# Four places of a two-layer backbone rewritten: key latents, adaLN rows and tanh moved, output weights asked for ahead, last tile scaled by two engines

## The chip, the cores and the metric

The kernel runs on one core of one Trainium2 chip. A core has five engines that run their own instruction lists and meet through semaphores: TensorE (PE: matmuls and transpositions), VectorE (DVE), ScalarE (ACT), GpSimd (POOL) and SyncE (SP), which here issues the DMAs. The metric is the device time of one execution in microseconds (us). All times are from the profiler's records or the timed runs.

## The reference

The program is one inference step of a diffusion backbone with two layers, on 256 context tokens (prompt) and 1024 latent tokens (sample), model width 1024. Cut to what matters:

```python
for l in (0, 1):
    shift, scale, gate = split(silu(cond) @ w_mod[l] + b_mod[l])     # "adaLN", for c_ctx and for c
    h = rmsnorm(y, norm_g[l]) * (1 + scale) + shift
    if l == 0:        # AB: windowed attention and a two-way matrix memory
        qa, ka, va, za, qb, kb, vb, ob, zb, gb = split(h @ w_in_ab)
        a = window_attention(rope(qa), rope(ka), va, cache, sink) * silu(za)
        qb, kb = split(silu(conv3([qb, kb])))                        # a centred convolution of 3 tokens
        b = norm(sigmoid(ob) * (memory_forward + memory_backward)) * silu(zb)
        out = concat(a, b) @ w_out_ab                                # 2048 x 1024
    else:             # C: attention over low-rank latents
        qa, kva, kr, z = split(h @ w_in_c)                           # 384, 256, 32, 1024 wide
        q = rmsnorm(qa) @ w_qb;  c_kv = concat(rmsnorm(kva), cache)
        k, v = split(c_kv @ w_kvb);  k = [k, rope(kr)]               # 16 heads
        out = (attention(q, k, v) * silu(z)) @ w_out_c               # 1024 x 1024
    y = y + gate * out
y_prompt, y_sample = rmsnorm(y, final_norm)                          # and the caches and states
```

## The kernel before

Matrices are kept as a high and a low half of an fp32 value (names ending in `h` and `l`), so that a product takes three matmuls: high by high, high by low, low by high. A product's weights are cast to the high half on ScalarE and the low half is a subtraction on VectorE or POOL. Tokens are handled in three chunks of 512, 512 and 256 (`CHUNKS`), or in ten tiles of 128 (`NT`).

The Python code lists the work; a scheduler that imitates the engines then lays out each engine's own order, and the order of each engine is fixed from there on. `K.later(f, n)` puts off a step by n steps of the surrounding flow, and `K.behind[(pass, tile)]` names what is to be issued beside a tile of a dense block. Memory on the chip is taken in pools, from a left and a right end (`left(...)`, `right(...)`); a new pool that lies over a released one waits for whoever last read there.

The places of the change, in the order of time:

- **adaLN rows** (`mod_sums`, line 501). Beside the first layer's work, the second layer's shift and scale are computed in blocks: 32 small matmuls, a ScalarE multiply into `mrow1` (L514, `mrow` in the profile), a transposition on PE, an addition on VectorE (L521).
- **The convolution of the memory branch** (`conv` in `b_proj`). ScalarE multiplies by the middle tap, VectorE adds the outer taps (L1629, L1630), ScalarE takes a tanh (L1632), VectorE finishes the silu (L1636), and the result `cx`, of which there are 4 buffers, is stored.
- **The output weights of layer AB** (`load_wout`, line 1009; `out_tile` uses them). They come one by one: a DMA on SP's queue, four steps later the cast (L1018) and the subtraction (L1019).
- **Key latents of layer C** (`kv_latent`, `k_rope`, `q_rope`, line 2020 on). `dense.run(2)` runs the last dense blocks of layer C's input product over the normalized input `hh0..2`, `hl0..2`. Query latents (`q_latent`) and the queries' rotary parts are placed beside it through `K.behind`. After it, the pool of the inputs is released, a pool `lat` is laid over it, and `kv_latent` for four chunks transposes the key latents and splits them into `ckv`, each with a `q_rope`.
- **Attention of layer C** (`Mla`). Eight pairs of heads; for each pair keys, queries and values are computed from `ckv`, the values of a pair into three tiles out of seven (`cV0` to `cV6`, three in the left pool `catt`, four in the right pool `cvr`). `SLOTS` says which: pair 7, the last, uses tiles 0, 2 and 1.
- **Output of layer C** (`weights_out`, `out`). The weights k = 0 to 2 go to a left pool (`cq`); before k = 3 the pools `cvr`, `ckv0`, `cw` and `lat` are released, and a pool `fin` over them takes k = 3 to 7 (`w`, L2183 and L2184), `fn`, `gate` and `o_x`. These steps and the first four output tiles are listed as filling for pair 7. An output tile is loaded (`o_a`), split (`o_ah`, `o_al`, L1056 and L1057), multiplied (48 matmuls), gated, added to `o_x`, squared and summed on ScalarE (L2205), and scaled by the root of the mean (L720, L721, L2216).

```python
SLOTS = ((3, 4, 5), (0, 1, 2), (3, 5, 0), (4, 6, 1), (0, 2, 4), (3, 5, 1), (4, 6, 3), (0, 2, 1))
```

Of the kernel before, what the change touches and what calls it, by code (L numbers as in the profile page):

```python
# [220 lines left out]
class Startup:  # L221
# [279 lines left out]
def mod_sums(K, p, blocks):  # L501


    nc, cond = K.nc, cond_cols(K, p)
    at = lambda t, c: t[c::32]
    if any(f < 2 * D for _, f in blocks):
        bcol = K.t(p, [128, 16], F32, "bcol1", 1)
        K.dma(bcol, K.I["k_cols"][:, 96:112])
        nc.vector.tensor_scalar(bcol[:, 8:16], bcol[:, 8:16], 1.0, None, ALU.add)
        K.A[1], K.Bm[1] = [K.const.tile([128, 2, 8], F32, tag=f"{n}1", name=f"{n}1") for n in "AB"]  # L510

    def columns(ps, f):
        rows = K.t(p, [128, 128], F32, "mrow1", 2)
        nc.scalar.mul(rows, ps[:, 0:128], 0.5)  # L514
        pc = K.psT()
        K.tr(pc[:, 0:128], rows)
        a, k = f // D, f % D // 128
        src = pc[:, 0:128].rearrange("p (q r) -> p q r", r=32)[:, :, 0:2]
        dst = (K.A if a else K.Bm)[1][:, :, k:k + 4].rearrange("p c k -> p k c")
        bc = lambda t, o: t[:, o + k:o + k + 4].unsqueeze(2).to_broadcast([128, 4, 2])  # L520
        nc.vector.tensor_add(dst, src, bc(bcol, 8 * a))  # L521
        if a:
            nc.vector.tensor_mul(dst, dst, bc(K.gcol, 8))

    def gate(ps, l, f, bias):
        nc.vector.scalar_tensor_tensor(bias, ps[:, 0:128], 0.5, bias, ALU.mult, ALU.add)
        for c in range(2):
            K.dma(K.modd[l][c, f:f + 512].rearrange("(q p) -> q p", p=128), at(bias, c))

    for l, f in blocks:  # L530
        ws, bias = [], None
        for i in range(8):
            for k in (2 * i, 2 * i + 1) if i < 4 else ():
                w = K.t(p, [128, 512], F32, "mw", 8)
                K.dma(w, K.I["w_mod"][l, k * 128:(k + 1) * 128, f:f + 512])
                ws.append(w)
            if i == 4 and f >= 2 * D:
                bias = K.t(p, [128, 128], F32, "bmod", 2)
                nc.gpsimd.memset(bias, 0.0)
                for c in range(2):  # L540
                    K.dma(at(bias, c), K.I["b_mod"][l, f:f + 512].rearrange("(q p) -> q p", p=128))
            if i == 7:
                ps = K.ps()
                for k in range(KD):
                    for q in range(4):
                        K.mm(ps[q * 32:q * 32 + 32, 0:128], cond[:, k, :], ws[k][:, q * 128:(q + 1) * 128], k == 0, k == KD - 1)
                if bias is None:
                    columns(ps, f)
                else:
                    gate(ps, l, f, bias)  # L550
# [299 lines left out]
def layer_ab(K):  # L850
# [158 lines left out]
def load_wout(K, p, src, ks, given=()):


    nc = K.nc
    K.wbufs = 2 * (len(ks) - len(given)) + (1 if len(ks) == 6 else 2)
    out = []

    def split(i, wf, half=None):
        wh, wl, wf = [t if half is None else t[:, half * 512:half * 512 + 512] for t in (*out[i], wf)]
        nc.scalar.copy(wh, wf)  # L1018
        (nc.gpsimd if K.flow or i % 3 else nc.vector).tensor_sub(wl, wf, wh.bitcast(F32))  # L1019

    def begin(i, wf):
        out.append(given[i] if i < len(given) else [K.t(p, [128, D], F32R, "w", K.wbufs) for _ in range(2)])
        if K.flow:
            split(i, wf, 0)
            K.later(partial(split, i, wf, 1))
        else:
            split(i, wf)

    for i, k in enumerate(ks):
        wf = K.t(p, [128, D], F32, "w", K.wbufs)  # L1030
        def ask(i=i, k=k, wf=wf):
            K.dma(wf, src[k * 128:(k + 1) * 128, :])
            K.later(partial(begin, i, wf), 4)

        K.later(ask, 1 + 3 * i)
    return out


# [556 lines left out]
def b_proj(K, wp, h):  # L1595
# [26 lines left out]
    def conv(p, ci, qk, j):  # L1622
        t0, N = CHUNKS[ci]
        cw = K.cw[:, :, qk * 8 + 2 * h + j]
        x = K.t(K.cvp, [128, 512], F32, "cx", 4)[:, 0:N]
        nc.scalar.mul(x, p[:, 1:N + 1], cw[:, 1:2])

        def taps():
            nc.vector.scalar_tensor_tensor(x, p[:, 0:N], cw[:, 0:1], x, ALU.mult, ALU.add)  # L1629
            nc.vector.scalar_tensor_tensor(x, p[:, 2:N + 2], cw[:, 2:3], x, ALU.mult, ALU.add)  # L1630
            th = K.sc(K.ring, [128, 512], F32, "cth")[:, 0:N]
            nc.scalar.activation(th, x, AF.Tanh, scale=1.0 if qk == 0 else 16.0)  # L1632
# [441 lines left out]
def layer_c(K):  # L2074
# [119 lines left out]
    def out(tt):  # L2194
        p = fin["p"]
        if tt in (0, 8):
            fin["gate"] = gate_row(K, p, 1, tt // 8)
        src = d["aT"][tt // 2][:, :, (tt % 2) * 128:(tt % 2) * 128 + 128]
        dst = K.O["y_sample"][0, tt * 128:(tt + 1) * 128] if tt < 8 else K.O["y_prompt"][0, (tt - 8) * 128:(tt - 7) * 128]
        ss = K.t(p, [128, 4], F32, "fss", 3)  # L2200
        if not tt:
            K.t(p, [128, 40], F32, "fpad", 1)

        def square(sl, y, x):
            nc.scalar.activation(x[:, sl], y[:, sl], AF.Square, accum_out=ss[:, sl.start // 256:sl.start // 256 + 1])  # L2205

        y = out_tile(K, p, [(src, 0, 4), (src, 4, 8)], fin["w"], fin["gate"], K.y2[tt], 4, square, fast=tt == NT - 1)
        if not tt:
            K.t(p, [128, 40], F32, "gpad", 1)
        nc.vector.tensor_add(ss[:, 0:1], ss[:, 0:1], ss[:, 2:3])  # L2210
        if tt == NT - 1:
            nc.vector.tensor_add(ss[:, 0:1], ss[:, 0:1], ss[:, 3:4])
        r = rstd_of(K, p, ss[:, 0:1], D, EPS, "fr")
        for n in range(0, D, 512):
            sl = slice(n, n + 512)
            nc.vector.scalar_tensor_tensor(y[:, sl], y[:, sl], r[:, 0:1], fin["fn"][:, sl], ALU.mult, ALU.mult)  # L2216
            K.dma(dst[:, sl], y[:, sl])
# [12 lines left out]
class Mla:  # L2230
# [298 lines left out]
```

## Time and profile before

| | us |
|---|---|
| median of three runs | 2583.2 (2578.94 to 2584.51) |
| the profiled execution | 2580.0 (2579.96) |
| its span in the profile | 2578.2 |
| PE busy in it | 2534.9 (98%) |
| mean granted PE clock | 0.996 |

The prediction shows the rows that it rests on. In the timeline a row is: start (us from the span's start), length, engine, line, operation, `out<-in`, shape, how many instructions were merged, and in brackets how long the engine stood idle just before and who released it. The page's waits are "engine tile line <- engine tile line: us in total, times, longest". A row of windows gives the length, the busy time of PE, PEld, DVE, ACT and POOL with the number of instructions, the granted PE clock, the DMA engines' mean busy share and GB/s.

### The profile page before, as it was taken

To read this page: it belongs to the slowest core of one execution; us is meant where nothing else is said; L and a number is where in the kernel's file an instruction comes from. 1 tells how busy PE (TensorE), PEld (TensorE's weight loads), DVE (VectorE), ACT (ScalarE), POOL (GpSimd) and SP (SyncE) were. 2 spreads that over 40 slices of the span, in tenths; PEclk is the share of its full clock that TensorE was granted. 3 is DMA by queue.
4 is the path that set the end of the run, shared out by engine and by line. 5 is a ranking of instruction groups with operands and counts; after the bars stand their busy time and mean duration, and the time that the engine had idled before them with its cause. 6 is when DMAs were issued, how large, how long until landed. Compare 5 with 4: busy or idle time off the path is not lost.

```text
span 2578.2 us, 48626 instructions
## 1 busy us (share of the span) xinstructions
PE 2534.9 (98%) x16482; PEld 2248.8 (87%) x16482; DVE 1702.8 (66%) x3927; ACT 1442.0 (56%) x3664; POOL 1126.9 (44%) x1510
## 2 busy tenths in 40 slices
PE   8999999999999999999999999999999999999998
PEld 6998998998998888878888778898899999999887
DVE  6633655656657575677777456426888888888754
ACT  6423535535434432577666433233888888888842
POOL 6223233233225344366554543135455555555832
PEclk9999999999999999999999999999999999999999
DMA  7665576666577564465443455423210101101334
GB/s 267 209 196 162 155 215 180 182 202 178 160 220 225 182 215 150 113 171 161 127 124 97 162 160 165 126 70 120 66 39 28 43 28 43 33 30 28 122 100 133
DMA packets 338955, 347.21 MB, mean 135 GB/s; under 512 B 36409, under 2 KB 281838, under 8 KB 338450
## 3 DMA queue, kind: packets, MB, share of 16 engines
q1 hardware_dynamic: 338706, 344.10, 43.8%
q8 instruction: 131, 2.15, 0.3%
q14 instruction: 118, 0.97, 0.1%
HBM read 233.49 MB, written 110.50 MB: 133 GB/s over the span
## 4 chain that ended last, share of the span: by engine, by line
PE 89%; DVE 3%; DMA 2%; ACT 2%; issue 2%; POOL 1%; SPq 1%; POOLq 0%; DVEq 0%; ACTq 0%
PE mm L119 36%; PE S L119 31%; PE V L119 9%; PE T L123 7%; PE D L119 3%; PE mm L123 3%; PE T L119 1%; SPq L154 1%; POOL w L1068 0%; DMA w<-in_w_out_c 0%; DMA w<-in_w_out_ab 0%; DMA y<-w 0%; POOL wl L577 0%; DMA xin<-in_x_sample 0%; DVE gM L1535 0%
## 5 line engine op out<-in xcount | busy, mean ns | idle before, releaser
L577 POOL TENSOR_TENSOR wl<-wf,wh 128x256 fp32r<-128x256 f32 (+2 forms) x272 | 222.8, 845 | 496.7 <-ACT wh L576 432.9
L119 PE MATMUL mm<-hTh,wh 128*128 128x512 f32 (+1 forms) x912 | 329.2, 361 | 0.9 <-DVE scr L821 0.9
L119 PE MATMUL mm<-hTh,wl 128*128 128x512 f32 (+1 forms) x912 | 324.7, 356 | 0.0
L119 PE MATMUL mm<-hTl,wh 128*128 128x512 f32 (+1 forms) x912 | 324.1, 355 | 0.0
L119 PE MATMUL S<-cK,cQ 96*128 96x512 f32 (+3 forms) x1248 | 301.6, 365 | 0.8 <-ACT cPb L2421 0.4
L2469 DVE TENSOR_TENSOR cpl<-T,cph 128x512 fp32r<-128x512 f32 x336 | 227.8, 684 | 36.3 <-ACT cph L2468 32.5
L119 PEld LDWEIGHTS S<-cK,cQ 96*128 96x128 f32 (+1 forms) x1248 | 192.5, 189 | 20.7 <-ACT cPb L2421 1.7
L2468 ACT CAST cph<-T 128x512 fp32r<-128x512 f32 x336 | 192.4, 589 | 29.1 <-PE T L123 15.7
L119 PEld LDWEIGHTS mm<-hTh,wl 128*128 128x128 f32 x912 | 171.4, 188 | 27.0
L119 PEld LDWEIGHTS mm<-hTh,wh 128*128 128x128 f32 x912 | 171.5, 188 | 23.8 <-DVE scr L821 1.1
L119 PEld LDWEIGHTS mm<-hTl,wh 128*128 128x128 f32 x912 | 171.7, 188 | 23.2
L2419 DVE TENSOR_REDUCE cmx<-S 128x1 f32<-128x512 f32 x256 | 172.9, 682 | 20.6 <-PE S L119 18.9
L119 PE MATMUL V<-cph,cV 128*128 128x256 f32 x672 | 177.3, 289 | 1.0 <-ACT cph L2468 0.9
L119 PE MATMUL V<-cpl,cV 128*128 128x256 f32 x672 | 171.9, 284 | 0.8 <-DVE cst L2396 0.3
L1343 ACT CAST att_ph<-mm 128x512 fp32r<-128x512 f32 x168 | 98.6, 587 | 94.4 <-PE mm L123 92.6
L2400 POOL TENSOR_SCALAR cPa<-cPa,cst 128x512 f32<-128x512 f32 x128 | 98.3, 768 | 114.5 <-DVE cst L2397 94.3
L119 PE MATMUL mm<-wh,hTh 128*128 128x256 f32 x480 | 136.2, 284 | 3.3 <-DVE scr L1649 3.2
L1344 DVE TENSOR_TENSOR att_pl<-mm,att_ph 128x512 fp32r<-128x512 f32 x168 | 115.8, 689 | 35.7 <-ACT att_ph L1343 30.8
L119 PE MATMUL mm<-wl,hTh 128*128 128x256 f32 x480 | 135.7, 283 | 0.1
L119 PE MATMUL mm<-wh,hTl 128*128 128x256 f32 x480 | 135.2, 282 | 0.0
L119 PEld LDWEIGHTS V<-cph,cV 128*128 128x128 f32 x672 | 126.6, 188 | 7.9 <-ACT cph L2468 1.1
L119 PEld LDWEIGHTS V<-cpl,cV 128*128 128x128 f32 x672 | 126.7, 189 | 6.7 <-DVE cpl L2469 0.9
(459 smaller groups left out, 7737.1 us busy)
## 6 DMA issues: line engine op xcount, KB each, us to landing
wf<-in_w_in_ab SPq DMA_DIRECT2D x120, 256.0 KB
in<-in SPq DMA_DIRECT2D x40, 514.0 KB
in<-in SPq DMA_DIRECT2D x32, 386.0 KB
mw<-in_w_mod SPq DMA_DIRECT2D x48, 256.0 KB
in<-scr SPq DMA_DIRECT2D x40, 258.0 KB
o_x<-y SPq DMA_DIRECT2D x20, 512.0 KB
xin<-in_k_wmod SPq DMA_DIRECT2D x16, 512.0 KB
in<-cx SPq DMA_DIRECT2D x32, 256.0 KB
```

The source lines that it names most:

```text
L119: return self.nc.tensor.matmul(out, lhsT, rhs, start=start, stop=stop)
L123: self.nc.tensor.transpose(out, in_, self.ident[:p, :p])
L154: self.nc.sync.dma_start(f(out), f(in_))
L577: K.nc.gpsimd.tensor_sub(wl, wf[:, k], wh.bitcast(F32))
L1343: K.nc.scalar.copy(ph, self.T)
L1344: K.nc.vector.tensor_sub(pl, self.T, ph.bitcast(F32))
L2400: nc.gpsimd.tensor_scalar(pv, pv, wt[:, c:c + 1], rd, ALU.mult, ALU.mult)
L2419: nc.vector.tensor_reduce(mx[:, b, c:c + 1], S, AX.X, ALU.max, negate=True)
L2468: nc.scalar.copy(ph, T_)
L2469: nc.vector.tensor_sub(pl, T_, ph.bitcast(F32))
```

## The change

1. `mod_sums` no longer transposes right behind ScalarE's multiply: the transposition and addition (`turned`) are kept and done when the next block has come to its third step.
2. The tanh of the convolution is put off by one step of the flow.
3. `load_wout` is a plain loop. It asks for two loads first and for one more ahead of each cast; the first load is on SP's queue, the others on ScalarE's.
4. Three of the four `kv_latent`, and eight `q_rope`, are spread beside the dense block. The pool `lat` is now the one that held `hh0` and `hl0`: the key latents are views of two tiles of their shape, and the fourth view of each becomes a value tile (`spare`). These are tiles 0 and 1 of the seven; three follow in `catt`, and `cvr` holds two.
5. In the last output tile the sums are folded into two small VectorE steps, and the second half is multiplied by `fn` on POOL beforehand, scaled on ScalarE and stored from ScalarE's queue.

```diff
@@ mod_sums
         nc.scalar.mul(rows, ps[:, 0:128], 0.5)
+        return partial(turned, rows, f)
+
+    def turned(rows, f):
         pc = K.psT()
         K.tr(pc[:, 0:128], rows)
...
+    late = None
     for l, f in blocks:
         ws, bias = [], None
         for i in range(8):
+            if i == 2 and late:
+                late = late()
...
-                    columns(ps, f)
+                    late = columns(ps, f)
...
+    if late:
+        late()
@@ dense blocks of layer C
+    K.lat = right("hT1")
+    hp = K.hp1 = right("hT2")
...
     for ci, (t0, N) in enumerate(CHUNKS):
+        hp = K.hp1 if ci else K.lat
@@ load_wout
+    nc, n = K.nc, len(ks)
+    K.wbufs = 2 * n + 1
+    out, raw = [], []
+
+    def ask(i):
+        if i < n:
+            raw.append(K.t(p, [128, D], F32, "w", K.wbufs))
+            (K.dma_act if i else K.dma)(raw[i], src[ks[i] * 128:(ks[i] + 1) * 128, :])
+
+    for i in range(2):
+        ask(i)
+    for i in range(n):
+        ask(i + 2)
+        wh, wl = [K.t(p, [128, D], F32R, "w", K.wbufs) for _ in range(2)]
+        out.append([wh, wl])
+        nc.scalar.copy(wh, raw[i])
+        (nc.gpsimd if i % 3 else nc.vector).tensor_sub(wl, raw[i], wh.bitcast(F32))
@@ conv
+            K.later(tanh)
+
+        def tanh():
             th = K.sc(K.ring, [128, 512], F32, "cth")[:, 0:N]
@@ layer_c
+    def keys_latent(ci):
+        if not ci:
+            for t, nm in zip(ckv, ("hh0", "hl0")):
+                whole = K.t(K.lat, [128, KD, 512], F32R, nm)
+                t += [whole[:, k:k + 2, :] for k in range(0, KD, 2)]
+        kv_latent(K, ci, ckv)
...
-    for n in range(8):
-        K.behind[1, n + 2] = [partial(q_rope, K, wr, n % 4, n // 4)]
-    K.behind[1, 5].append(partial(k_rope, K, 0))
-    K.behind[1, 9].append(partial(k_rope, K, 1))
+    for n, at in enumerate(((0, 7), (0, 8), (1, 0), (1, 2), (1, 3), (1, 4), (1, 6), (1, 8))):
+        K.behind.setdefault(at, []).append(partial(q_rope, K, wr, n % 4, n // 4))
+    for f, ci, at in ((k_rope, 0, (1, 5)), (k_rope, 1, (1, 9))):
+        K.behind.setdefault(at, []).append(partial(f, K, ci))
+    for ci, tt in ((0, 5), (3, 7), (1, 9)):
+        K.behind.setdefault((1, tt), []).append(partial(keys_latent, ci))
...
-    lp = right("lat")
-    ckv = [[lp.tile([128, 2, 512], F32R, tag=f"ckv{s}{c}", name=f"ckv{s}{c}") for c in range(3)] for s in range(2)]
+    lp = K.lat
+    spare = [t.pop().rearrange("p k (i g a d) -> p (k i) g a d", i=2, g=2, a=2) for t in ckv]
...
-    for ci in range(4):
-        kv_latent(K, ci, ckv)
-        q_rope(K, wr, ci, 2)
+    kv_latent(K, 2, ckv)
+    for q in range(4):
+        q_rope(K, wr, q, 2)
...
-    C.add_values(ap, sets[1])
+    C.add_values(ap, sets[1], spare=spare)
@@ out, last tile
+            if tt == NT - 1 and sl.start:
+                nc.gpsimd.tensor_mul(yf[:, sl.start - 512:sl.stop - 512], y[:, sl], fin["fn"][:, sl])
...
+            nc.vector.scalar_tensor_tensor(y[:, 0:512], y[:, 0:512], r[:, 0:1], fin["fn"][:, 0:512], ALU.mult, ALU.mult)
+            nc.scalar.mul(yf, yf, r[:, 0:1])
+            K.dma(dst[:, 0:512], y[:, 0:512])
+            K.dma_act(dst[:, 512:1024], yf)
@@ add_values
-        tiles = []
-        for pool, k in zip(pools, (3, 4)):
+        tiles = [*spare]
+        for pool, k in zip(pools, (3, 2)):
```

Since the scheduler sets the order, three places of the engines' orders show what moved.

PE, the first of the adaLN rows beside the first layer, before (`S` is a matmul's sum of a dense unit, `T` a transposition; the leading numbers of the names are buffers):

```order
L119 MATMUL S_1939<-wl_1484,hTh_127 128x256
L119 MATMUL S_1939<-wh_1483,hTl_128 128x256
L119 MATMUL S_1939<-wh_1487,hTh_127 128x256
L123 MATMUL T_2017<-ident,mrow_366_2015 128x128
L119 MATMUL S_1939<-wl_1488,hTh_127 128x256
L119 MATMUL S_1939<-wh_1487,hTl_128 128x256
```

and in the change:

```order
L119 MATMUL S_2076<-wh_1487,hTl_130 128x256
L123 MATMUL T_2106<-ident,mrow_366_2015 128x128
L119 MATMUL S_2113<-wh_1455,hTh_129 128x256
L119 MATMUL S_2113<-wl_1456,hTh_129 128x256
L119 MATMUL S_2113<-wh_1455,hTl_130 128x256
```

The transposition stands 38 rows later on PE, between two units. The two after it move by 38 and 26 rows, the fourth not at all.

SP's queue, the first of the last output weights, before (`caT` and `csz` belong to the gating of the attention's output; in brackets the engines and queues that a DMA waits for):

```order
L154 DMA caT_4176_19543<-csz_31419 128x256 [waits DMAHW4_49,Pool_49]
L154 DMA csz_31797<-csz_4172_19539 128x256 [waits DMAHW5_49,DMAHW4_49]
L154 DMA w_31947<-in_w_out_c 128x512 [waits DVE_49]
L154 DMA w_31974<-in_w_out_c 128x512 [waits DMAHW3_49,Activation_49]
L154 DMA w_32009<-in_w_out_c 128x512 [waits DMAHW0_49]
L154 DMA fn<-in_final_norm 128x1024 [waits DVE_49,PE_49]
L154 DMA gate_32362<-modd_54_144 128x1024 [waits DMAHW2_49]
L154 DMA o_x_32366<-y_0_469_2786 128x1024
L154 DMA w_32035<-in_w_out_c 128x512 [waits DVE_49]
```

and in the change:

```order
L154 DMA caT_4176_19546<-csz_32889 128x256 [waits Pool_49]
L154 DMA w_31941<-in_w_out_c 128x512 [waits DMAHW7_49,DVE_49,PE_49]
L154 DMA w_31968<-in_w_out_c 128x512 [waits PE_49]
L154 DMA w_32003<-in_w_out_c 128x512 [waits DMAHW1_49]
L154 DMA fn<-in_final_norm 128x1024
L154 DMA gate_32356<-modd_54_144 128x1024 [waits DMAHW3_49]
L154 DMA o_x_32360<-y_0_469_2786 128x1024 [waits DVE_49,PE_49]
L154 DMA w_32029<-in_w_out_c 128x512 [waits DMAHW5_49]
L154 DMA w_32062<-in_w_out_c 128x512 [waits DMAHW6_49,Activation_49]
L154 DMA o_a_32363<-caT_4173_19543 128x4x128 [waits DMAHW7_49]
```

Three loads now wait for PE: the first for values of pair 6 in `cV4`, the second for the matmuls of `V_33122` that read `hh_4699`, `o_x` for the last matmul of `V_33211` below. The store of `caT` ahead of them is that of pair 7's fourth tile, where before it was pair 6's.

PE at the end of the attention, in the change (`V` are the products with the values, of which `hh` and `hl` are the spare tiles; `mm<-cq,o_ah` is the first output tile):

```order
L119 MATMUL V_33122<-cph_33182,hl_4700_22307 128x256
L119 MATMUL V_33122<-cpl_33183,hl_4700_22307 128x256
L119 MATMUL V_33193<-cph_33199,hl_4700_22307 128x256
L119 MATMUL V_33193<-cpl_33200,hl_4700_22307 128x256
L119 MATMUL V_33211<-cph_33217,hl_4700_22307 128x256
L119 MATMUL V_33211<-cpl_33218,hl_4700_22307 128x256
L119 MATMUL mm_32375<-cq_31750,o_ah_32365 128x512
L119 MATMUL mm_32375<-cq_31751,o_ah_32365 128x512
L119 MATMUL mm_32375<-cq_31750,o_al_32366 128x512
```

All 480 matmuls of the output tiles stand behind the last `V` now. Before, 234 of the 480 stood among pair 7's attention, and the other 246 behind it.

More of the change, by code (lines that the diff above doesn't have):

```diff
@@ L962, in layer_ab @@
         opened.pop().release()
-    hp = K.hp1 = right("hT1")
+    K.lat = right("hT1")
+    hp = K.hp1 = right("hT2")
     K.hTh, K.hTl = [], []
     for ci, (t0, N) in enumerate(CHUNKS):
+        hp = K.hp1 if ci else K.lat
         K.hTh.append(hp.tile([128, KD, N], F32R, tag=f"hh{ci}", name=f"h1Th{ci}"))
@@ L1006, in place_wout, with load_wout @@
         yield
[L1009 to L1035, printed above, removed]
+def load_wout(K, p, src, ks):
+    nc, n = K.nc, len(ks)
[13 more added lines that the diff above has]
+        (nc.gpsimd if i % 3 else nc.vector).tensor_sub(wl, raw[i], wh.bitcast(F32))
     return out
@@ L2119, in layer_c @@
     K.u = {}
-    K.behind = {(0, 5): [partial(q_latent, K, 0)], (0, 9): [partial(q_latent, K, 1)], (1, 1): [partial(q_latent, K, 2)]}
-    for n in range(8):
-        K.behind[1, n + 2] = [partial(q_rope, K, wr, n % 4, n // 4)]
-    K.behind[1, 5].append(partial(k_rope, K, 0))
-    K.behind[1, 9].append(partial(k_rope, K, 1))
+    ckv = [[], []]
+    def keys_latent(ci):
[4 more added lines that the diff above has]
+        kv_latent(K, ci, ckv)
+    K.behind = {(0, 5): [partial(q_latent, K, 0)], (0, 9): [partial(q_latent, K, 1)], (1, 1): [partial(q_latent, K, 2)]}
+    for n, at in enumerate(((0, 7), (0, 8), (1, 0), (1, 2), (1, 3), (1, 4), (1, 6), (1, 8))):
[4 more added lines that the diff above has]
+        K.behind.setdefault((1, tt), []).append(partial(keys_latent, ci))
     dense.run(2)
@@ L2202, in out @@
             K.t(p, [128, 40], F32, "fpad", 1)
+        yf = K.t(p, [128, 512], F32, "fyf", 1) if tt == NT - 1 else None
         def square(sl, y, x):
             nc.scalar.activation(x[:, sl], y[:, sl], AF.Square, accum_out=ss[:, sl.start // 256:sl.start // 256 + 1])
+            if tt == NT - 1 and sl.start:
+                nc.gpsimd.tensor_mul(yf[:, sl.start - 512:sl.stop - 512], y[:, sl], fin["fn"][:, sl])
         y = out_tile(K, p, [(src, 0, 4), (src, 4, 8)], fin["w"], fin["gate"], K.y2[tt], 4, square, fast=tt == NT - 1)
@@ L2209, in out @@
             K.t(p, [128, 40], F32, "gpad", 1)
+        if tt == NT - 1:
+            nc.vector.tensor_scalar(ss[:, 2:3], ss[:, 2:3], ss[:, 0:1], D * EPS, ALU.add, ALU.add)
+            nc.vector.tensor_scalar(ss[:, 3:4], ss[:, 3:4], ss[:, 2:3], 1.0 / D, ALU.add, ALU.mult)
+            r = K.t(p, [128, 1], F32, "fr", 4)
+            nc.gpsimd.tensor_tensor(r, ss[:, 3:4], K.mhalf, ALU.pow)
+            nc.vector.scalar_tensor_tensor(y[:, 0:512], y[:, 0:512], r[:, 0:1], fin["fn"][:, 0:512], ALU.mult, ALU.mult)
+            nc.scalar.mul(yf, yf, r[:, 0:1])
+            K.dma(dst[:, 0:512], y[:, 0:512])
+            K.dma_act(dst[:, 512:1024], yf)
+            return
         nc.vector.tensor_add(ss[:, 0:1], ss[:, 0:1], ss[:, 2:3])
-        if tt == NT - 1:
-            nc.vector.tensor_add(ss[:, 0:1], ss[:, 0:1], ss[:, 3:4])
         r = rstd_of(K, p, ss[:, 0:1], D, EPS, "fr")
@@ L2250, in add_set, with add_values @@
         self.KV.append(keys)
-    def add_values(self, *pools):
+    def add_values(self, *pools, spare):
         n = 0
-        tiles = []
-        for pool, k in zip(pools, (3, 4)):
+        tiles = [*spare]
+        for pool, k in zip(pools, (3, 2)):
             tiles += [pool.tile([128, 4, 2, 2, 64], F32R, tag=f"cV{i}", name=f"cV{i}") for i in range(n, n + k)]
```

## The prediction

> **What bounds the kernel now.** I read the page first, then the waits of the tensor engine (PE), then single places in the timeline.
>
> ```profile
> PE 2534.9 (98%) x16482; PEld 2248.8 (87%) x16482; DVE 1702.8 (66%) x3927; ACT 1442.0 (56%) x3664; POOL 1126.9 (44%) x1510
> PE T L123 <- ACT mrow L514: 5.0, 2, 4.6
> PE mm L119 <- DVE scr L1649: 3.2, 1, 3.2
> PE T L123 <- DVE ckv L2071: 1.8, 4, 0.6
> ```
>
> PE is busy for 2534.9 of 2578.2 us. The change neither adds nor removes a matmul of any weight, so only what PE loses can move: idle time, the slower pace after it, and the end. The three waits shown (total, times, longest) are those that the edits aim at; a fourth is below.
>
> **The adaLN rows.** The transposition of `mrow` sat in the middle of a group of matmuls, and PE stood before it.
>
> ```profile
> 142.73 0.25 ACT L514 ACTIVATE mrow<-S 128x128 f32<-128x128 f32 x1
> 143.04 0.48 PE L123 MATMUL T<-ident,mrow 128*128 128x128 f32 x1 [4.59 <-ACT mrow L514]
> 143.74 0.41 PE L119 MATMUL S<-wh,hTh 128*128 128x256 f32 x1
> 143.95 0.41 PE L119 MATMUL S<-wl,hTh 128*128 128x256 f32 x1
> 149.03 0.28 PE L119 MATMUL S<-wh,hTl 128*128 128x256 f32 x1
> 149.14 0.28 PE L119 MATMUL S<-wh,hTh 128*128 128x256 f32 x1
> 147.33 1.27 ACT L1567 ACTIVATE rst<-rst 36x1280 f32<-36x1280 f32 x1
> 153.80 0.79 PE L123 MATMUL T<-ident,rst 36*128 36x36 f32 x10
> ```
>
> Two things were lost: 4.59 us of standing, and after it some 25 matmuls that started 0.21 us apart instead of 0.11 to 0.12, which is 25 x 0.094 = 2.3 us: 6.9 in all. Now 38 matmuls stand ahead of the transposition, 38 x 0.118 = 4.5 us, so PE reaches it at about 142.8, when `mrow` (142.98) is all but there. What is late next: the transposition of `rst` stood at 153.80 and comes 6.9 us earlier, at 146.9, but ScalarE's exponential ends at 147.33 + 1.27 = 148.60, and nothing in the edit moves that. PE waits some 2 us there; the gain is 153.80 - 148.8 = 5.0, less 0.3 for the restart: **4.7**, bounds 0 (the wait only moves) and 6.9.
>
> In the Trainium skill, "TensorE: Matmul & The Clock Gate" (Part 1: The HAM clock gate) has the array fall to half its clock after an idle window of about 3.4 us and come back after one busy window. The rows here agree in kind (0.21 against 0.11 to 0.12), though the slow stretch was longer, 143.04 to 148.65. By the page's window a wait of 2 us would not slow the array, and the sum would gain the 0.3 that I took off.
>
> **tanh one step later.** One wait, in a chain of four.
>
> ```profile
> 678.53 0.75 DVE L1630 SCALAR_TENSOR_TENSOR cx<-scr,cw,cx 128x512 f32<-128x512 f32 x1
> 679.32 0.63 ACT L1632 ACTIVATE scr<-cx 128x512 f32<-128x512 f32 x1 [0.75 <-DVE cx L1630]
> 680.24 0.42 DVE L1649 TENSOR_TENSOR scr<-mm,scr 128x256 fp32r<-128x256 f32 x1 [0.36 <-ACT scr L1648]
> 680.72 0.39 PE L119 MATMUL mm<-wh,hTh 128*128 128x256 f32 x1 [3.22 <-DVE scr L1649]
> ```
>
> The tanh waited for VectorE, and the cast and subtraction that free PE's bank stood behind it. With the tanh of the convolution before in its place, ScalarE is 0.75 us early; but the store of `cx` also goes one step later, and a later convolution reuses that buffer, so ScalarE's multiply must wait for the store. Of 3.22 us I take **1.1**; bounds -1 (that new wait is the longer one) and 4.9 (the wait and its slow pace both go). Elsewhere the 39 tanh's wait on ScalarE alone, and PE doesn't follow it.
>
> **The last output weights, asked for ahead.**
>
> ```profile
> 1456.99 8.73 DMA w<-in_w_out_ab
> 1476.45 1.05 ACT L1018 CAST w<-w 128x1024 fp32r<-128x1024 f32 x1 [6.00 <-DMA w<-in_w_out_ab]
> 1478.81 0.50 PE L119 MATMUL S<-w,o_ah 128*128 128x512 f32 x1 [0.30 <-DVE w L1019]
> 1483.12 0.50 PE L119 MATMUL S<-w,o_ah 128*128 128x512 f32 x1 [0.83 <-POOL w L1019]
> ```
>
> The loads landed one at a time, and PE paid 0.30 + 0.83 us, and in the matmuls around (0.50 us each against 0.39 at full pace, as below) about as much again. Asked two ahead, all six are under way earlier. But now ScalarE waits for a landing with the casts of `o_ah` behind it, and PE waits for those: up to 1 us. I take **1.5**, bounds -1 and 2.5. The Trainium skill ("Trainium Kernel Development and Optimization", Key Constraints) says that DMAs of several engines' queues run on the same 16 DMA engines, and that a second queue saves only the issuing time; no load here is issued by ScalarE before. By that rule the asking ahead alone would count, and this edit would bring nearer 0 than 1.5.
>
> **Key latents beside the dense block.**
>
> ```profile
> 1680.00:1740.00 60.00, 60.00 (x385) 59.00 (x384) 13.57 (x33) 25.11 (x64) 22.75 (x28) 1.00 0.29 70
> 1786.70:1801.00 14.30, 10.84 (x39) 7.34 (x38) 9.07 (x19) 7.63 (x17) 9.24 (x12) 0.76 0.51 157
> 1794.92 1.22 PE L119 MATMUL S<-ckv,wkh 128*128 128x512 f32 x2 [0.64 <-DVE cK L2068]
> 1798.50 0.63 PE L119 MATMUL mm<-cq,wql 128*128 128x512 f32 x1
> 1798.93 1.06 PE L119 MATMUL mm<-cq,wqh 128*128 128x512 f32 x2
> 1801.60 0.39 PE L119 MATMUL S<-ckv,wkl 128*128 128x512 f32 x1
> 1801.82 0.39 PE L119 MATMUL S<-ckv,wkh 128*128 128x512 f32 x1
> ```
>
> The first two rows are windows: length, busy us of PE, PEld, DVE, ACT and POOL, granted clock, DMA share and GB/s. In the 14.30 us of the second PE did 16 transpositions (0.11 each, about the step of the 256-column matmuls above) and 21 matmuls of 512 columns, which start 0.22 to 0.23 us apart at full pace (1801.60 to 1801.82): 1.8 + 4.8 = 6.6 us of work, so 7.7 were lost, to waits and to the slow pace (0.43 us from 1798.50 to 1798.93). Three of the four chunks now run among the dense block's matmuls, where PE was never idle (60.00 of 60.00) and VectorE and ScalarE had room; only the last keeps 4 transpositions here, with nine matmuls of `cq` as cover. **7.0**; bounds 4 (the last chunk still slows the clock) and 7.7.
>
> **The last tile.** After the last matmul came, in a row:
>
> ```profile
> 2572.74 0.16 DVE L2212 TENSOR_TENSOR fss<-fss 128x1 f32<-128x1 f32 x1 [0.57 <-ACT o_x L2205]
> 2573.82 1.42 DVE L2216 SCALAR_TENSOR_TENSOR w<-w,fr,fn 128x512 f32<-128x512 f32 x2 [0.73 <-POOL fr L721]
> 2574.60 1.00 SPq L154 DMA_DIRECT2D out_y_prompt<-w  x2
> ```
>
> One small VectorE step (0.2) goes; the second half is scaled and issued beside the first, half of 1.42 us and the second issue: **1.0**, bounds 0 and 2.
>
> **What the change puts in the way.** The key latents of chunk 0 stay in the old tile of `hh0`/`hl0`, and the spare quarter of each becomes a value tile. The last head pair reads them to the end, and the pool with the last output weights (`w<-in_w_out_c`, k = 3 to 7), `fn`, `gate` and `o_x` lies over that space. So the second of these loads waits for the last but one group of attention matmuls, `o_x` for the very last one, and the rest of SP's queue stands behind. In PE's order all 480 matmuls of the output come after the attention. Before, 234 of them were woven into it.
>
> ```profile
> 2401.90 1.37 SPq L154 DMA_DIRECT2D w<-in_w_out_c  x3
> 2404.74 9.24 DMA w<-in_w_out_c
> 2404.97 0.62 ACT L2183 CAST w<-w 128x512 fp32r<-128x512 f32 x1 [0.45 <-DMA w<-in_w_out_c]
> 2404.98 0.74 POOL L2486 TENSOR_TENSOR csz<-co,csz 128x256 f32<-128x256 f32 x1
> 2414.00 0.62 ACT L2183 CAST w<-w 128x512 fp32r<-128x512 f32 x1 [0.27 <-DMA w<-in_w_out_c]
> 2419.86 3.77 POOL L2184 TENSOR_TENSOR w<-w,w 128x512 fp32r<-128x512 f32 x3
> GB/s 0 0 125 0 166 259 283 254 244 285 218 339 367 390 380 359 226 312 46 183 70 12 2 232 16 0 0 47 78 45 265 231 82 0 0 23 212 28 11 0
> 2340.00:2404.00 64.00, 63.63 (x437) 57.29 (x435) 55.77 (x129) 57.30 (x159) 39.83 (x64) 1.00 0.15 44
> 2404.00:2435.00 31.00, 29.63 (x200) 26.23 (x201) 23.27 (x53) 27.72 (x74) 28.45 (x38) 1.00 0.54 171
> 2520.00:2571.00 51.00, 51.00 (x246) 42.54 (x245) 22.22 (x40) 12.04 (x29) 14.91 (x13) 1.00 0.44 146
> ```
>
> Attention without output matmuls keeps PE busy (63.63 of 64.00), so the new order costs nothing until the attention ends. Call that end t. The store that heads SP's queue follows a ScalarE copy (under the 0.62 of a cast twice as wide), a POOL product (0.74) and its issue, and begins from the group that ends 1 us before t: the first load is issued at about t + 1.2. The seventh issue, the second half of k = 4, came 2404.74 - 2401.90 = 2.8 us after the first and took 9.24 to land: t + 13.3. Its cast takes 0.62, and POOL's subtractions 3.77 / 3 = 1.26 each. The load of the first half of k = 7 must wait for the second of these (t + 16.4) for its buffer, then 3.1 us (2401.90 to 2404.97), 0.6 and 1.3: t + 21.5, and three matmuls more make t + 22.2. The 24 matmuls of that first group cost 24 x 0.225 = 5.4 us anyway: **PE loses 16.8**. To this come 1.2 for the last attention chain, which has no other work beside it, and 1.0 for a slow pace that POOL doesn't hide. Off goes 2.5 for the stretch 2404 to 2435, where loading disturbed the attention (29.63 busy of 31.00, and a slower pace). Sum: **a loss of 16.5**. Bounds: 10 if the loads, alone on the engines, land at the 390 GB/s that this stretch reached at best (the GB/s row, 40 slices from 2398 to 2440; the seven loads, four of 256 KB and three of 512, are 2.6 MB, 6.7 us instead of about 10.5), with the rest 2 us better for it, and 23 if the load of k = 7 takes 9.24 us instead of 3.1.
>
> **The sum.** Gains 4.7 + 1.1 + 1.5 + 7.0 + 1.0 = 15.3, loss 16.5: 1.2 us more than the profiled execution's own 2580.0 (span 2578.2), 2581.2. The median of the three runs is 3.2 us above that execution, which gives 2584.4; I take the middle, **2583**.
>
> **The rivals.**
> 1. *The loads land sooner* (faster). Nothing else uses the DMA engines after t. For it: the window 2404 to 2435 shows attention's own traffic beside the loads. Against it: 9.24 us from issue to landing came while the DMA engines were mostly this queue's. With a loss of 10 and all the gains: 2583 - 6.5 = 2576.5.
> 2. *The buffer decides* (slower). The load of k = 7 is asked for only when POOL has freed a buffer, and stands behind a load of `o_a` that waits for VectorE. It decides once that load takes over about 5 us to land. For it: POOL is the slowest link of the chain, and these loads landed in 3 to 9 us. Against it: by then little else is queued. Price 6.1: 2583 + 6 = 2589.
> 3. *The gains at the start and in the key latents are half* (slower). At both the stall may move to the next producer, as `rst` shows. 2583 + 6 = 2589 as well.
> 4. *The move does not bite*: the loads wait in SP's order, yet come before PE needs them, because attention ends late. The order speaks against it: the waits name the last matmuls. 2583 - 16.5 = 2566.5.
>
> **How the numbers follow.** Between two kernels here a difference under 0.2%, 5.2 us, can't be told from none. My forecast, no difference to be told, gets 0.42; the first rival 0.22 and the fourth 0.05; the second and third 0.31 together. So faster 0.27, same 0.42, slower 0.31. The forecast's own range is 2578 to 2588. The 8-in-10 range reaches to the first rival and to the second and third: **2573 to 2591**.
>
> **What would show it.** Right: at the end of attention PE idle for 12 to 15 us until `o_ah`, with the ten `w<-in_w_out_c` loads issued within some us behind it; no wait for `mrow` above 0.5 us; 1 to 2 us before `rst`; the stretch of the key latents 6 to 7 us shorter. Wrong: output loads issued some 100 us before the end as now, a wait of PE for a cast of `o_ah` near 1461, or new gaps among the dense matmuls before 1786.

## The result, and the profile after

| | before | the change |
|---|---|---|
| median | 2583.2 us (2578.94 to 2586.23, 5 runs) | 2607.88 us (2606.84 to 2609.08, 5 runs) |
| ratio, 95% interval | | 1.0099 (1.0084 to 1.0113) |
| span of the profiled execution | 2578.2 us | 2606.1 us |
| PE busy in it | 2534.9 us | 2537.9 us |

The change is 24.7 us slower, outside the range of the prediction (2573 to 2591). PE is busy for 3.0 us more than before, so of the 27.9 us between the spans 24.9 are idle time and the rest is slower pace. That kind of loss is what the prediction had; how much of it, and where, came out otherwise. One run of the kernel before, beside e5 to e7 below, took 10443.5 us and is in no ratio.

Rows of PE's waits, of the change (total us, times, longest):

```profile
PE mm L119 <- ACT o_ah L1059: 12.3, 1, 12.3
PE mm L119 <- DVE w L1070: 5.8, 7, 0.9
PE T L123 <- DVE B L524: 4.0, 1, 4.0
PE mm L119 <- DVE scr L1655: 3.5, 1, 3.5
PE V L119 <- DVE co L2513: 2.8, 3, 1.5
PE mm L119 <- DVE rp_t L829: 2.4, 1, 2.4
PE S L119 <- DMA mw<-in_w_mod: 1.9, 3, 0.9
PE S L119 <- POOL o_al L1432: 1.6, 1, 1.6
PE S L119 <- ACT o_ah L1431: 1.4, 1, 1.4
```

Of the three waits that the edits aimed at only `scr` is there in its old form (`mrow` is down from 5.0 to 0.4), and each has a successor: `mrow` became `B`, `ckv` became `rp_t`, the wait for the output weights `w` became two waits for `o_ah` and `o_al`. The first, second and fifth row are the end of the program, which had none of them before.

To see where the time went, the start of the same matmul is compared in both profiles. The table gives PE's lag behind the kernel before in us (minus: PE is ahead), worked out from the traces of the change and of the experiments below (e1 to e7), at places where the same work has been done:

| place (time before) | change | e1 | e2 | e3 | e4 | e5 | e6 | e7 |
|---|---|---|---|---|---|---|---|---|
| first transposition of the gates' rows (120) | +4.8 | +0.1 | +0.6 | +0.2 | +0.8 | -0.1 | +1.2 | +0.3 |
| gates done (183) | +4.6 | +1.7 | +0.3 | -1.0 | +0.4 | -3.2 | +0.2 | -3.0 |
| memory branch, behind the tanh place (732) | +5.5 | -0.3 | -1.6 | 0.0 | -1.4 | -2.9 | +1.7 | -3.0 |
| attention of the first layer ends (1445) | +5.7 | -0.1 | -1.5 | -0.9 | -1.2 | -2.9 | +1.3 | -1.5 |
| output of the first layer done (1640) | +4.8 | +2.3 | -0.7 | -2.7 | -0.8 | -3.7 | +0.9 | -3.2 |
| first keys by queries (1815) | -0.4 | -2.8 | -4.2 | -7.6 | -3.4 | -4.8 | -0.1 | -8.4 |
| second layer, early pairs (2132) | +2.9 | +1.8 | -1.1 | -4.2 | -0.4 | -4.6 | -0.1 | -6.2 |
| last matmul (2571) | +27.8 | +1.6 | +18.2 | -3.5 | +2.1 | -3.1 | -0.3 | -5.6 |

The first row is not the change's doing: up to that place the orders of PE and of SP's queue are the same in both kernels. In this one execution some `mw` loads came late (the row `mw<-in_w_mod` above); among the other eight profiles only e4 has such a wait, of 0.2 us. So of the 27.8 us, 4.8 are chance; whether the other four timed runs had such a delay isn't known. On the way from there to 2132 the change won 1.9 (4.8 to 2.9), not the 14 that I had summed. e2 has the same orders in this stretch, and e1 too but for the numbers of two value tiles: e2 won 1.7 in it, and e1 lost 1.7. Together the three show no gain clear of chance. The rest, 24.9, came behind 2132, all of it at the end.

**The end.** Two windows of the change there, then its timeline: SP's queue, ScalarE, POOL, PE and VectorE:

```profile
2434.00:2466.00 32.00, 28.70 (x222) 26.72 (x220) 25.08 (x58) 24.11 (x64) 15.16 (x27) 1.00 0.08 24
2466.00:2478.00 12.00, 0.05 (x1) 0.05 (x1) 0.49 (x2) 3.85 (x8) 6.07 (x6) 0.50 0.97 325
2464.47 1.34 SPq L154 DMA_DIRECT2D w<-in_w_out_c  x3
2475.71 1.33 ACT L2200 CAST w<-w 128x512 fp32r<-128x512 f32 x2 [5.11 <-DMA w<-in_w_out_c]
2477.28 0.62 ACT L1059 CAST o_ah<-o_a 128x512 fp32r<-128x512 f32 x1 [0.24 <-DMA o_a<-caT]
2476.41 7.12 POOL L2201 TENSOR_TENSOR w<-w,w 128x512 fp32r<-128x512 f32 x5 [4.46 <-ACT w L2200]
2483.89 1.28 POOL L2201 TENSOR_TENSOR w<-w,w 128x512 fp32r<-128x512 f32 x1 [0.36 <-ACT w L2200]
2477.95 1.22 PE L119 MATMUL mm<-cq,o_ah 128*128 128x512 f32 x2 [12.28 <-ACT o_ah L1059]
2485.52 0.62 PE L119 MATMUL mm<-w,o_ah 128*128 128x512 f32 x2
2486.45 0.69 DVE L1070 TENSOR_TENSOR w<-mm,gate 128x512 f32<-128x512 f32 x1 [5.31 <-PE mm L119]
2487.20 0.73 PE L119 MATMUL mm<-cq,o_ah 128*128 128x512 f32 x2 [0.84 <-DVE w L1070]
2493.86 0.70 PE L119 MATMUL mm<-cq,o_ah 128*128 128x512 f32 x2 [0.88 <-DVE w L1070]
```

The output loads go out at 2464.47, where before it was 2401.90, and PE stands for 12.28 us until the first `o_ah` is cast. That is what the prediction described. The output tiles are 504 matmuls by the trace (48 of the last tile are half as wide), not 480; before, 258 of them stood among the attention and 246 behind it, and now all stand behind. What the prediction had not: after each group of 24 matmuls PE pauses again, until VectorE has multiplied the sum by `gate` and so emptied the bank (L1070). The first four output tiles use the one bank of the pool `mm`. While their matmuls stood among the attention, other work covered this; now there is none, seven times.

### The profile page after: what moved, and what is told of

The parts are those of the page before. It is cut to its first block, busy times and chain, and to the rows that moved or that the text cites. A ratio compares the mean times of both kernels' runs of the same rounds, so it can differ in the third digit from the quotient of the medians.

```text
span 2606.1 us, 48638 instructions
## 1 busy us (share of the span) xinstructions
PE 2537.9 (97%) x16482; PEld 2250.5 (86%) x16482; DVE 1698.4 (65%) x3925; ACT 1441.1 (55%) x3665; POOL 1131.9 (43%) x1512
## 4 chain that ended last, share of the span: by engine, by line
PE 85%; DVE 3%; DMA 2%; issue 2%; ACT 2%; POOL 1%; SPq 1%; POOLq 0%; ACTq 0%; DVEq 0%
PE mm L119 34%; PE S L119 30%; PE V L119 9%; PE T L123 7%; PE D L119 3%; PE mm L123 3%; PE T L119 1%; SPq L154 1%; DMA o_a<-bT 0%; DMA o_a<-caT 0%; DVE cmx L2448 0%; DVE w L1070 0%; DVE att_pl L1347 0%; DMA out_new_cache_a_k<-scr 0%; DVE att_nm L1321 0%
## 5 line engine op out<-in xcount | busy, mean ns | idle before, releaser
L1335 POOL TENSOR_SCALAR att_p<-att_p,att_den 128x640 f32<-128x640 f32 (+1 forms) x128 | 97.9, 780 | 80.3 <-DVE att_den L1332 27.5
L584 ACT CAST wh<-wf 128x256 fp32r<-128x256 f32 (+2 forms) x272 | 96.2, 409 | 60.3 <-DMA wf<-in_w_in_c 24.0
L119 PE MATMUL V<-cph,cV 128*128 128x256 f32 x464 | 123.6, 289 | 0.0
L119 PE MATMUL V<-cpl,cV 128*128 128x256 f32 x464 | 119.3, 284 | 0.8 <-DVE cst L2422 0.3
```

Source lines behind the costliest of these rows:

```text
L119: return self.nc.tensor.matmul(out, lhsT, rhs, start=start, stop=stop)
L584: K.nc.scalar.copy(wh, wf[:, k])
L1335: nc.gpsimd.tensor_scalar(pv, pv, den[:, i:i + 1], 1.0, ALU.mult, ALU.mult)
```

## The experiments

The kernel before was run again beside each set, with medians of 2580.5 (e1 to e4) and 2582.4 us (e5 to e7); the ratios are to those.

**e1: the value tiles elsewhere.** One line of the change:

```diff
-        tiles = [*spare]
+        tiles = []
         for pool, k in zip(pools, (3, 2)):
             tiles += [pool.tile([128, 4, 2, 2, 64], F32R, tag=f"cV{i}", name=f"cV{i}") for i in range(n, n + k)]
             n += k
+        tiles[3:3] = spare
```

> The change with one line moved: the two spare value tiles are numbers 3 and 4 of the seven instead of 0 and 1, so that the last head pair (tiles 0, 2, 1) has all its values in the left pool and nothing of it under the pool of the output weights. Theory (that overlap is the tail's loss): the output loads are issued some 100 us before the end again, more than 200 of the 480 output matmuls stand among the last pair's attention, the 12.3 us wait for o_ah and the waits for DVE L1070 go; 2607.9 - 27.9 = 2580, between 2576 and 2585. Rival (the moved latents and the new pool layout as such delay the end): above 2600.

Measured: 2580.6 us, ratio 1.0001 (0.9991 to 1.0010). The first of the output loads on its SP queue, and all of PE's waits behind 2400:

```profile
2403.50 1.33 SPq L154 DMA_DIRECT2D w<-in_w_out_c  x3
```

```profile
PE V L119 <- ACT cph L2498: 0.9, 1, 0.9
PE V L119 <- DVE cpl L2499: 0.3, 1, 0.3
PE T L123 <- DVE cpl L2499: 0.2, 1, 0.2
```

The loads are 61 us earlier than in the change, and 12.3 + 5.8 + 2.8 us of waits are gone. They are issued 176 us before the end of the program, where the expectation had said some 100, and 258 of the output matmuls stand among the attention again. With the same moved latents, the whole loss goes with the place of two tiles. The rival falls.

**e2: three banks for the output tiles**, all else as in the change:

```diff
-               (24, partial(out, 0)), (29, partial(out, 1)), (34, partial(out, 2)), (39, partial(out, 3))])
+               ])
     C.finish()
     K.ps = K.psS
-    for tt in range(4, NT):
+    for tt in range(NT):
         out(tt)
```

> The change, with the first four output tiles taking their sums from the three banks of S, as the other six do, instead of the single bank of mm. Theory (seven pauses of PE after the attention are waits for VectorE to empty that one bank, 0.78 to 0.88 us each and about 1.0 with the restart): 2607.9 - 7 = 2601, between 2599 and 2604; the 12.3 us wait for o_ah stays. Rival (the pauses are the arrival of weights or the slow clock): within 2 us of 2607.9.

Measured: 2598.35 us, ratio 1.0074 (1.0057 to 1.0091), where the change had 1.0099: against the kernel before, 17.8 us in place of 24.7, so 6.9 less. That is 0.65 us below the stated range, which was reckoned from 2583.2 for the kernel before, while beside e2 that kernel took 2580.5. PE's waits from 2440 on:

```profile
PE S L119 <- ACT o_ah L1059: 13.5, 1, 13.5
PE V L119 <- DVE co L2513: 2.8, 3, 1.5
PE T L123 <- DVE cpl L2498: 0.2, 1, 0.2
```

The seven pauses are gone and the wait for `o_ah` stays. By the table e2 loses 19.3 us behind 2132, against 24.9. So the one bank is some 6 to 7 us of the loss, as the theory has it, and the rival falls.

**e3 and e4: the key latents alone, and all the rest alone.** e3 is the kernel before with the latents' part of the diff and the tile numbers of e1; e4 is the change without that part.

> The kernel before with the key latents' move alone, the spare value tiles as numbers 3 and 4. Theory (5.1 us are won up to the first product of keys and queries, and about 3.2 of it is given back in new waits for queries and keys behind it): 2583.2 - 1.9 = 2581, between 2577 and 2585. Rival (the term of the prediction holds, 7.0): 2576.

> The change without the key latents' move: adaLN rows, tanh, output weights asked ahead and last tile. Theory (the wait for mrow only moves to the transposition of rst, which waits for its bank; tanh costs about 1; the weights and the last tile bring nothing): 2583.2 + 1 = 2584, between 2580 and 2588. Rival (the terms of the prediction, 4.7 + 1.1 + 1.5 + 1.0): 2575.

Measured: e3 2580.57 us, 0.9997 (0.9988 to 1.0007); e4 2583.39 us, 1.0011 (1.0002 to 1.0021). Neither reaches the prediction's terms. Of e4's lag of 2.1 us at the last matmul, 2.5 is one wait for a cast of `cph` at 2408.79, a place that its edits don't touch. The table shows where e3's gain goes: from -2.7 at 1640 (up to there e3 has no edit, so that is chance) to -7.6 at the first keys by queries (4.9 won, 7.0 predicted), and back to -4.2 at 2132. The waits that take it back, in the change:

```profile
1797.26 0.70 PE L119 MATMUL mm<-cq,wqh 128*128 128x512 f32 x2 [2.43 <-DVE rp_t L829]
1822.78 0.47 PE L119 MATMUL mm<-hh,wkh 128*128 128x512 f32 x1 [1.45 <-DVE cQ L2074]
```

2.43 us remain at the old place, since the last rotary part still goes through VectorE before PE can go on, and another 1.45 come where the attention starts. Both stand in e3 as well. e4 leaves the latents where they were. Its window over the old place, and its own wait at the start of the attention:

```profile
1786.70:1801.00 14.30, 10.73 (x50) 7.50 (x50) 8.82 (x18) 7.82 (x18) 8.45 (x11) 1.00 0.53 168
1819.70 0.44 PE L123 MATMUL T<-ident,cPa 128*128 128x128 f32 x2 [1.45 <-POOL cPa L2416]
```

It had won 2.6 us from 1640 to the first keys by queries, too (-0.8 to -3.4), with the same four waits for `ckv` as before (1.8 us) but a granted clock of 1.00, where the kernel before had 0.76: that gain goes with the clock. It gave 3.0 back by 2132. So the profiles that gain between 1640 and the start of the attention wait there; e5, whose lead is older, keeps it (-4.8 to -4.6). What sets that pace stays open.

**e5: the adaLN rows behind the gates**, on the kernel before:

```diff
-            if i == 2 and late:
+            if i == 4 and late:
```

> The kernel before with the adaLN rows alone, but put off to the next block's fifth step instead of its third, so that the transposition of mrow stands on PE behind the three of the gates (LI, rst, gM) and not ahead of them. Theory (in the change the transposition of rst waits, beyond ScalarE's exponential, for the bank that the transposition of mrow left full: its emptying, L524, stands on VectorE behind four subtractions that wait for ScalarE's casts): rst then waits for the exponential alone, PE stands some 2 us there, and PE's lead over the kernel before behind the gates is 4 to 5 us, where it is 0 in the change; the time is 4 to 5 us below the kernel before. Rival (PE cannot be early there at all, because the gate chain on VectorE sets the pace): no lead behind the gates, and no difference in time.

Measured: 2578.57 us, 0.9985 (0.9976 to 0.9994): 3.8 us below. The two kernels at the transposition of `rst`, first the change:

```profile
152.15 1.27 ACT L1570 ACTIVATE rst<-rst 36x1280 f32<-36x1280 f32 x1
153.99 1.42 ACT L1654 CAST scr<-S 128x256 fp32r<-128x256 f32 x5
154.09 1.41 DVE L1655 TENSOR_TENSOR scr<-S,scr 128x256 fp32r<-128x256 f32 x4
155.49 0.16 DVE L524 TENSOR_TENSOR B<-T,bcol 128x8 f32<-128x8 f32 x1
155.80 1.25 PE L123 MATMUL T<-ident,rst 36*128 36x36 f32 x10 [4.02 <-DVE B L524]
```

and e5:

```profile
147.24 1.27 ACT L1575 ACTIVATE rst<-rst 36x1280 f32<-36x1280 f32 x1
148.56 0.81 PE L123 MATMUL T<-ident,rst 36*128 36x36 f32 x10 [1.78 <-ACT rst L1575]
```

In the change the exponential of `rst` was done at 153.42, but PE went on at 155.80, when VectorE had emptied the bank of `mrow` (L524), behind four subtractions, behind ScalarE's casts. With the transposition put behind the gates, PE waits 1.78 us for the exponential and nothing else. PE's lead behind the gates is 3.2 us (3.0 in e7), a little below the 4 to 5 expected. The theory holds, with its size somewhat too large; the rival falls.

**e6: one queue**, for the output weights and the last tile of the change on the kernel before:

```diff
-            (K.dma_act if i else K.dma)(raw[i], src[ks[i] * 128:(ks[i] + 1) * 128, :])
+            K.dma(raw[i], src[ks[i] * 128:(ks[i] + 1) * 128, :])
...
-            K.dma_act(dst[:, 512:1024], yf)
+            K.dma(dst[:, 512:1024], yf)
```

> The kernel before with the output weights asked for two ahead and the last tile as in the change, but all their loads and stores on SP's queue. Theory (what hurts in the change is not the queue: ScalarE's cast waits for a landing with the casts of o_ah behind it, and two stores at once share the DMA engines): PE waits again 2.5 to 3.5 us for o_ah and o_al near 1462 to 1467, and from the last matmul to the end it is 7.2 to 7.5 us. Rival (ScalarE's queue is the cause): no wait there above 0.5 us, and the end 1 us shorter, 6.2.

Measured, in one run, too few for a verdict on the time: 2579.48 us. At the output weights the theory fell. The change, on ScalarE's queue:

```profile
1462.48 1.05 ACT L1037 CAST w<-w 128x1024 fp32r<-128x1024 f32 x1 [7.59 <-DMA w<-in_w_out_ab]
1467.07 0.33 ACTq L157 DMA_DIRECT2D w<-in_w_out_ab  x1
1467.50 1.04 ACT L1037 CAST w<-w 128x1024 fp32r<-128x1024 f32 x1 [3.02 <-DMA y<-o_y]
1468.91 0.50 PE L119 MATMUL S<-hh,o_ah 128*128 128x512 f32 x1 [1.40 <-ACT o_ah L1431]
1471.74 0.49 PE L119 MATMUL S<-hh,o_al 128*128 128x512 f32 x1 [1.63 <-POOL o_al L1432]
```

and e6, the only wait of PE above 0.3 us from 1440 to 1545:

```profile
1491.06 1.20 PE L119 MATMUL S<-w,o_ah 128*128 128x512 f32 x4 [1.99 <-ACT o_ah L1049]
```

The two waits of PE belong to the queue: ScalarE stood 3.02 us until the store of `y` had landed, before one of its own DMAs, with the casts of `o_ah` behind it. All four profiles with the loads on ScalarE's queue have both waits (2.8 to 3.6 us together); on SP's queue they are gone. But the gain is not there either: a wait of 1.99 for another `o_ah` comes later, whose cast stands on ScalarE behind casts that waited 5.85 us for a load. From 1445 to 1640 the kernels with the old loads (e3, e5, e7) won 1.8, 0.8 and 1.7 us on the profile before, by chance; with the edit, the change won 0.9, and e1, e2 and e4 lost 2.4, 0.8 and 0.4. With the profile before counted as 0, that is a mean of 1.1 won against one of 0.7 lost: on ScalarE's queue the edit costs about 2 us there, with a spread of as much. e6, a single execution, won 0.4, so what the edit costs on SP's queue can't be told.

The last tile went nearly as the theory said: 7.06 us from the last matmul to the end, just below its 7.2 to 7.5 and far from the rival's 6.2. The change's end:

```profile
2601.53 0.72 ACT L2237 ACTIVATE fyf<-fyf,fr 128x512 f32<-128x512 f32 x1 [0.97 <-POOL fr L2235]
2602.28 0.38 ACTq L157 DMA_DIRECT2D out_y_prompt<-fyf  x1
2602.31 0.33 SPq L154 DMA_DIRECT2D out_y_prompt<-w  x1
```

Both halves are scaled 0.8 us sooner after the start of the last matmul than the second half was before (2602.28 - 2598.81 = 3.5, against 2575.24 - 2570.97 = 4.3). But the first store was issued 3.6 us after that start before (2574.60), and is 3.5 after it now; and from the first issue to the end it is 3.6 us before, 3.8 in the change and 3.6 in e6. In all three the DMA engines move the 0.52 MB of both stores without a gap, at 350 to 420 GB/s in most slices, so a second half that is ready sooner has to wait for the first. From the last matmul to the end: 7.21 before, 7.28 in the change, 7.06 in e6. The Trainium skill has the shared engines in "Trainium Kernel Development and Optimization", Key Constraints: DMAs of several queues run on the same 16 engines, and a second queue saves only issuing time. The trace agrees that it brings no more: with the second queue the end came 0.2 us later than in e6.

**e7: the best of it.** The kernel before with the rows as in e5, tanh one step later, and the latents as in e3.

> The kernel before with the adaLN rows put off to the fifth step, tanh one step later, and the key latents' move with the spare value tiles as numbers 3 and 4; output weights and last tile as before. Theory: 4.5 for the rows, 1.5 for tanh and 1 to 2 for the key latents, 7 us below the kernel before. Rival (each gain is eaten at the next wait): within 3 us of it.

Measured: 2575.34 us, 0.9974 (0.9964 to 0.9984): 6.7 us faster than the kernel before, and 32 faster than the change by the two ratios (2583 x (1.0099 - 0.9974)). The theory holds in sum, and the rival falls. Term by term it was partly luck: by the table the rows gave 3.3 (4.5 expected); tanh gave nothing (-3.0 to -3.0, 1.5 expected); the latents 3.0 from 1640 to 2132 (1 to 2 expected).

**tanh.** No run has it alone, but the profiles show what it did. ScalarE and PE in the change, then PE in e1:

```profile
679.44 0.72 ACT L1629 ACTIVATE cx<-scr,cw 128x512 f32<-128x512 f32 x1 [5.31 <-DMA in<-cx]
685.44 0.58 PE L119 MATMUL mm<-wh,hTh 128*128 128x256 f32 x1 [3.48 <-DVE scr L1655]
686.03 0.41 PE L119 MATMUL mm<-wh,hTl 128*128 128x256 f32 x1
```

```profile
682.00 0.38 PE L119 MATMUL mm<-wh,hTh 128*128 128x256 f32 x1 [2.99 <-DVE scr L1655]
682.22 0.28 PE L119 MATMUL mm<-wl,hTh 128*128 128x256 f32 x1
```

ScalarE now waits 5.31 us for the store of a `cx` whose buffer it needs, and the casts that free PE's bank are as late as they were: 3.48 and 2.99 us, against 3.22. What differs is the pace behind it: each matmul shows 0.41 us after 3.48, and 0.28 after 2.99. Over the place (183 to 732) the change lost 0.9 us, e1, e2 and e4 won 2.0, 1.9 and 1.8, e7 nothing; without the edit e3, e5 and e6 lost 1.0, 0.3 and 1.5. The last section has the pauses of all nine profiles.

## Why the prediction was wrong, point by point

Both sides of the sum failed. The gains, 15.3 in it, came to between 1.9 won and 1.7 lost in the three profiles that have the change's early edits, and to nothing at the last tile. The loss, 16.5 in it, came to 24.9. Of the signs that the prediction named, PE's standing for 12 to 15 us until `o_ah` is there (12.28); the wait before `rst` is 4.02 us and not 1 to 2; and a sign of being wrong is there too, the wait for a cast of `o_ah` (1.40 us at 1468.91).

- **The end: the mechanism right, its size too small (16.5 predicted, 24.9 measured).** The term that failed is what comes after the first group of output matmuls: nothing was put down for it. The window 2520 to 2571, in which PE is never idle, has tiles that use three banks; the first four tiles use one. That is about 7 us (e2). Second, the last attention chain was put at 1.2 and cost some 3.3 (28.70 busy of 32.00 us): the products with the values have one bank too, and the three waits for `co` are 2.8 of it. The wait itself was about right: from the last attention matmul (2465.7) to the end of the first group (2486.2) it is 20.5 - 5.4 = 15.1, predicted 16.8. But the sum took that length from the load of k = 7, and PE stood for `o_ah` (12.28) and then ran the group at a slow pace (2.8 more). The two chains nearly tie: the low half of k = 7 was done at 2485.17, 0.35 us before PE came to it. So the length agrees partly by luck. The first load was issued 1.2 us before the attention ended, not after. The relief of the stretch from 2404 on was about 2.4 (2.5): leaving the output matmuls out, PE's lag fell from 2.8 us at 2395 to 0.4 at 2428. 15.1 + 3.3 + 7 - 2.4 makes 23 of the 24.9; the rest isn't placed.
- **adaLN rows: 4.7 predicted, between 0.4 won and 1.6 lost in the four profiles that have them so.** The step "nothing in the edit moves that" failed. The place of the `rst` transposition that the sum named, 148.8, is where e5 has it (148.56). In the change, the moved transposition fills a bank that `rst` needs next, and the addition that empties it was moved too, behind VectorE's work. I followed the moved instruction on PE, not its successor on VectorE.
- **Key latents: 7.0 predicted, 3.5 to 5.2 at the place and 0.4 to 3.0 by 2132, in the five profiles that have them moved.** The chance of the last chunk (bound 4) was in the text. What was not is the give-back at the start of the attention, 2.2 to 4.6 us by the table. And the 7.7 us lost there were read from the execution with the slowest clock (0.76): e4, e5 and e6, whose latents stay, are 1.0 to 2.6 us faster over the place.
- **tanh: 1.1 predicted, between -0.9 and 2.0 measured.** The mean of the five is 1.0, but by luck: the casts come no earlier. The new wait for the store was named and is there (5.31 us of ScalarE); what the profiles gain or lose hangs on whether the clock falls behind the wait of PE, which is still there.
- **Output weights: 1.5 predicted, a loss of about 2.** The cause was named (casts of `o_ah` behind a wait of ScalarE, "up to 1 us"); it was 3.0. ScalarE waits not only for landings but for the space of what it asks for.
- **Last tile: 1.0 predicted, nothing.** The step that failed is the second issue, counted as if it came alone: the DMA engines were still moving the first store, and both take as long together.
- **The rivals.** The first (the loads land sooner) did not happen: the second half of k = 4, issued at 2467.27, let ScalarE go on at 2475.71, 8.4 us later (9.24 in the sum), with the DMA engines 0.97 busy at 325 GB/s. The second (the load of k = 7 decides) did not happen in its form: POOL's subtractions ran on, five in a row in 7.12 us, and k = 7 came just in time. The third (the gains at the start and in the latents move to the next producer) did. The fourth did not: PE stood 12.28 us. Both slower rivals together had 0.31; the sum of the true terms lies beyond either of them, since the gains failed and the loss grew at once.

## What to carry to other kernels

When a tile is given a second life, ask what will be laid over its memory and when its last reader is: one line that numbers two tiles cost 25 us here, at a place far from the edit, because a queue of loads stood behind that reader. Work that loses its neighbours must be priced with its own buffers: a single bank that costs nothing beside other work cost 0.8 to 0.9 us of standing at each of seven groups by itself. And a moved step takes its bank along: follow it to the instruction that empties the bank, on that engine's order, before crediting a wait as gone.

## What the runs showed of the hardware that I had not expected

At the tanh place all nine profiles have the same pause of PE, within 0.5 us, and it decides over 2 us of time. Counted in the traces: the pause, how many of the 29 matmuls after the first one ran at the slow step of 0.21 us in place of 0.12, when the slow steps began behind the pause, and when they ended.

| | e1 | e2 | e4 | e3 | before | e5 | e6 | e7 | change |
|---|---|---|---|---|---|---|---|---|---|
| pause, us | 2.99 | 3.04 | 3.16 | 3.20 | 3.22 | 3.22 | 3.23 | 3.27 | 3.48 |
| slow matmuls | 0 | 0 | 0 | 25 | 16 | 16 | 27 | 16 | 23 |
| slow from, us | | | | at once | 0.47 | 1.52 | at once | 0.93 | at once |
| slow until, us | | | | 5.71 | 3.88 | 4.92 | 6.12 | 4.31 | 5.29 |

Up to 3.16 us there is none, from 3.20 on there are 16 to 27. The 31 steps behind the pause take 3.74 us in the first three, 5.25 to 5.27 where 16 are slow and 6.13 to 6.46 where more are: 1.5 to 2.7 us. Where the slow steps begin late they last 3.38 to 3.41 us in all three. The change, e1 and e2 have the same order of PE up to there and yet show 3.48, 2.99 and 3.04: the execution alone tips it, and the tanh edit can't be credited or blamed by one profile. The Trainium skill ("TensorE: Matmul & The Clock Gate", Part 1: The HAM clock gate) describes a window of about 3.4 us that runs freely: the clock is halved after an idle one and restored after a busy one. The slow stretches of 3.4 us agree with the second. The pauses of 3.20 to 3.27 us that had slow steps behind them are shorter than that window, and here the measurement decides: at this place the limit lay between 3.16 and 3.20 us.

In the stretch of the key latents the clock fell with no pause above 0.7 us, as the granted clock of 0.76 and the steps of 0.43 us in the prediction show. That many short pauses do it is not shown: e4 has the same ones and a granted clock of 1.00.

And the same orders on the same engines differ between executions: in the first 120 us one profile, with late `mw` loads, lost 4.8 us, and the others at most 1.2. A sum made against one execution can't be expected to hold to better than that.
